# A two-layer trunk with top-2-of-8 experts on one core: the eight ranked experts run in the order of 64, 96, 64, 96, 64, 128, 96 and 32 slots instead of 128 first, the ring of weight buffers is cut down only around the 128, and the router drops twenty unread products

## The chip, the core and the metric

The kernel runs on one core of a Trainium2 chip. TensorE (PE) multiplies, VectorE (DVE) and ScalarE (ACT) do the element-wise work, GpSimd (POOL) a few small things, and SyncE (SP) issues every transfer from HBM. The metric is the time of one execution in microseconds of the device, as a median over runs. All times below are microseconds (us) from the start of the profiled span.

## The reference, cut to what matters

Layer 0 is an mLSTM and differential-attention mixer with a dense SwiGLU, layer 1 a convolution module and then a mixture of experts. The change touches the last part alone, over 256 tokens of width 1024:

```python
logits = (tokens @ router_w).astype(F32)
top_vals, top_idx = lax.top_k(logits, TOP_K)        # 2 of 8 experts for each token
gates = jax.nn.softmax(top_vals, axis=-1)
...
y = (jax.nn.silu(xb @ w1[e]) * (xb @ w3[e])) @ w2[e]   # hidden width 2816, for each expert e
out = jnp.zeros((N, D), y.dtype).at[slot_tok].add(y * slot_g)
```

All eight experts have weights of 1024 x 2816 three times over, in float32, and all are read from HBM.

## The kernel before, in words

**Ranks and slots.** The router counts how many tokens chose each expert (`counted`) and sorts the experts by that count (`ranks`). The expert of rank r gets `SLOTS[r]` places for tokens; what does not fit goes to a rare path (`overflow`) that is not taken here. Only after the sort is it known which weights belong to which rank: `bases` holds the place of each rank's weights, SP loads it into a register (L2049), and every transfer of expert weights stands behind that load on SP's queue.

**Order.** `TURNS` gives the order in which ranks are worked off, `GROUPS` which neighbours have their tokens gathered in one go. In before the widths in order of time are 128, 96, 64, 96, 64, 96, 64, 32.

**Units.** Weights come in units of 1 MB (128 x 2048 float32). An expert has 33: its hidden width is cut into six blocks (five of 512 columns, one of 256), and the order is four units of the first two matrices ("up") for a block, then two units of the third matrix ("down") for the block before it; the last block has two and one. The down unit of the last block comes behind the first four up units of the next expert. So, counting units from 0, the last up unit of the first block of expert i (i from 0) is number 3 for i = 0 and 33 i + 2 for i of 1 and more.

**Two ways to multiply.** With 128 slots (class `Expert`) each half unit is split by ACT (L371, a copy in reduced form, `whi`) and DVE (L372, the rest, `wlo`), and PE does three products per weight tile. The unit's buffer is free as soon as it is split. With fewer (class `Tiled`) PE reads the unit itself in float32, in slices of 64 (`wide`) or 32 (`narrow`) places that stand beside each other in the array. With 96 places both are done: the wide slice unit by unit, and the narrow one for all four up units only when the fourth has come (`held`), so that these four stay in use until then. ACT's Silu marks the end of a block's up products: L1809 in the 128, L1916 in the others (`cv` for the wide slice, `cvt` for the narrow one).

**The ring.** `room` is the list of buffers that successive units take: six `raw`, one made of `gp` and `m4`, three of the tag `B8`, which makes ten. While no expert is split, the four pairs of `whi` and `wlo` are used as buffers too, and a fourth `B8`: fifteen. SP issues in the order of units and stops at the first one whose buffer is still in use.

**The router's unread products.** `warm(n)` issues n products of 512 columns on PE whose result nobody reads.

The work on PE, DVE and ACT stands in the order of the code (`in_order`). The functions that the change touches:

Of the kernel before, what the change touches and what calls it, by code (L numbers as in the profile page):

```python
# [19 lines left out]
P = 128  # L20
# [6 lines left out]
NE = 8  # L27
# [5 lines left out]
AHEAD = 4  # L33

SLOTS = (128, 96, 96, 96, 64, 64, 64, 32)
TURNS = (0, 1, 4, 2, 5, 3, 6, 7)
GROUPS = ((0,), (1, 2), (3, 4), (5, 6), (7,))
NV = 2


# [195 lines left out]
def build(ctx: ExitStack, tc: tile.TileContext, d, unit, dbg=None):  # L236
# [41 lines left out]
    V, A, G, PE = nc.vector, nc.scalar, nc.gpsimd, nc.tensor  # L278
# [7 lines left out]
    def warm(n, bank="mm"):  # L286

        p_ = pm(bank)
        for _ in range(n):
            mm(p_.rearrange("p (r c) -> p r c", r=4), identr, identr.unsqueeze(1).to_broadcast([P, 4, P]), True, True)  # L290
# [36 lines left out]
    room = []  # L327
# [446 lines left out]
    for j2 in range(2):  # L774
# [4 lines left out]
        for j in range(2):  # L779
            i = 2 * j2 + j  # L780
            src = pq[:, T * j : T * j + T]
            w = cw[:, 3 * i : 3 * i + 3]
# [83 lines left out]
    for j2 in range(2):  # L866
        W = split(("k", j2))
        for j in range(2):
            pk = pm()
            wstat(W[j], pk, 0, S)  # L870
            i = 2 * j2 + j
            w = cw[:, 12 + 3 * i : 15 + 3 * i]
# [57 lines left out]
    for j2 in range(2):  # L930
# [7 lines left out]
        for j in range(2):  # L938
            i = 2 * j2 + j
            rope(qs[:, T * j : T * j + T], dqT[:, i, :])  # L940
    for j2 in range(2):
        W = split(("dk", j2))
        for j in range(2):
            i = 2 * j2 + j
# [604 lines left out]


    NU = unit[("m1", 1, 0, 0)] - unit[("m1", 0, 0, 0)]
    while len(room) < NU + 8:
        room += ["raw"] * 6 + ["gp"] + ["B8"] * 3
    while len(room) < NU * (NE - 1) - 6:
        room += ["raw"] * 6 + ["w"] * 4 + ["gp"] + ["B8"] * 4
    while len(room) < NU * NE - 13:
        room += ["raw"] * 6 + ["w"] * 4 + ["B8"] * 3
    xT_ = tl([P, KT, T], "B8")
# [169 lines left out]
    with in_order():  # L1728
        N = Norms(ys, gp)
        N.y(0, 0)  # L1730
        N.y(1, 0)
        N.y(0, 1)
        r = rms_inv(N.sy[0])
        N.add(0, 0, r)
        N.add(0, 1, r)
        rms_part(xt[:, 0, :512], N.sx[0][:, 0:1])
        N.y(1, 1, True)
        rms_part(xt[:, 0, 512:], N.sx[0][:, 1:2])
        warm(6)
        b0 = turned(xt[:, 0])  # L1740
        ry = rms_inv(N.sy[1])
        N.w_(1, 1)
        warm(3)
        b1 = turned(N.w[1])
        r0 = rms_inv(N.sx[0])
        A.copy(xT_[:, 0:4, 0:P], b0[0])
        A.copy(xT_[:, 4:8, 0:P], b0[1])
        A.copy(xT_[:, 4:8, P:], b1[1])
        warm(3)
        logits(0)  # L1750
        N.add(1, 0, ry)
        rms_part(xt[:, 1, :512], N.sx[1][:, 0:1])
        N.add(1, 1, ry)
        rms_part(xt[:, 1, 512:], N.sx[1][:, 1:2])
        V.tensor_copy(xT_[:, 0:4, P:], b1[0])
        warm(2)
        logits(1)
        r1 = rms_inv(N.sx[1])
        top2(0, r0, None)
        warm(4)  # L1760
        p0 = slots(0)
        top2(1, r1, ry)
        warm(2)
        pc = counted()
        p1 = slots(1)
        ranks(pc)
        warm(2)
        g0 = Group(0)
        p0()
        p1()  # L1770
        by_rank(posr, pos)
        g0.onehot(0)
        parts(0, 0, r0)
        g0.onehot(1)
        parts(1, 0, r1)
        parts(0, 1, r0)
        parts(1, 1, r1)
        i = g0.gather(range(2), V.tensor_copy)
    fence = fence_after(*i)
    dbg("x2", xt)  # L1780
    acc = None
# [349 lines left out]
    def later(n, *fns):  # L2131
        for i, fn in enumerate(fns):
            due.setdefault(len(todo) + n + i, []).append(fn)
# [40 lines left out]
    for i in range(NE):  # L2174
        x = ex[i]
        if i == 0:
            later(2, *[partial(g0.gather, (k,), V.tensor_copy) for k in (2, 3)])
            later(5, g0.turn)
            later(7, gates, first, partial(by_rank, gtr, gt))
            later(10, too_many)  # L2180
            later(30, left)
        for j in range(6):
            for h in range(2 if j < 5 else 1):
                if few(i):
                    todo.append(([("m1", i, j, h), ("m3", i, j, h)], None, partial(x.up2, j, h)))
                else:
                    for n in ("m1", "m3"):
                        for q in range(2):
                            todo.append(([(n, i, j, h)], q, partial(x.up, j, h, int(n == "m3"), q)))
            wait = 2 if (i, j) == (last, 5) and not few(i) else 1 if (i, j) in ((0, 0), (last, 5)) else 2 if few(i) else 3  # L2190
            later(0, partial(x.act, j))
            later(wait, partial(x.turn, j), partial(x.turned, j))
            if (i, j) == (last, 1):
                later(2, row)
            if (i, j) == (last, 3):
                later(1, slot_gate, *[partial(acc_parts, t, c) for t in range(TT) for c in range(2)])
            g = group_of.get(i + 1)
            if g is not None and g != group_of[i]:
                if j == 2:
                    later(0, partial(new_group, g), *[lambda g=g, t=t: groups[g].onehot(t) for t in range(TT)])  # L2200
                    later(3, lambda g=g: groups[g].turn())
                if j == 3:
                    later(1, *[lambda g=g, k=k: groups[g].gather((k,)) for k in range(4)])
            if j:
                downs(i, j - 1)
            elif i:
                downs(i - 1, 5)
# [100 lines left out]
```

## Time and profile before

| what | us |
|---|---|
| median of 3 runs (1324.64 to 1328.2) | 1326.01 |
| the profiled execution, its own time | 1329.66 |
| its span, from the first instruction to the last | 1327.9 |
| first transfer of expert weights issued | 604.79 |
| last expert unit used by PE | 1309.24 |

A row of the timeline has the start, the length, the engine, the line, what is written and what is read, how many instructions were merged, and in brackets how long the engine had been idle and what ended it. A product in plain float32 appears as two records. In the windows, PEclk is the granted clock of TensorE as a share of 2.4 GHz, and GB/s what the core's DMA engines moved.

### The profile page before, as it was taken

Reading aid. Unit: us, or ns where it says so; the run is one execution under the profiler, and the core shown is the slowest. Engines: PE = TensorE matmul, PEld = TensorE weight load, DVE = VectorE, ACT = ScalarE, POOL = GpSimd, SP = SyncE. Lnnn points to the kernel's source line nnn. Section 1 sums busy time; section 2 is a strip of 40 time slices with the busy share of each in tenths; the row PEclk is TensorE's granted clock in tenths of the full one; section 3 lists DMA queues with packets and bytes.
Section 4 is the critical chain, followed back from the end, with each engine's and each line's share of the span. In section 5 each row is a group of like instructions: output and inputs, shape, how many; then the busy total and the mean of one; then the engine's idle time right before and its main releaser. Section 6 shows DMA issues by size and latency. Waiting matters only on the chain. (4 is left out here: it accounts for less than half of the span.)

```text
span 1327.9 us, 21579 instructions
## 1 busy us (share of the span) xinstructions
PE 1234.6 (93%) x8655; PEld 793.5 (60%) x8655; DVE 635.7 (48%) x1055; ACT 432.9 (33%) x786; POOL 33.1 (2%) x72
## 2 busy tenths in 40 slices
PE   6999999989999998997999999999999899998654
PEld 4878777789998987686777434343343333433222
DVE  4589758698886668666977211201112021120102
ACT  4553246564434553264875001120011110110101
POOL 2000001100000010001000000000000000000000
PEclk8999999999999998996999999999999999999977
DMA  8728720478987627207987899999999999999974
GB/s 329 285 99 302 298 112 5 158 299 356 354 326 310 254 69 211 77 1 289 420 336 286 348 376 416 415 418 418 417 416 415 417 416 416 416 418 418 417 315 192
DMA packets 71518, 406.35 MB, mean 306 GB/s; under 512 B 7922, under 2 KB 12274, under 8 KB 32628
## 3 DMA queue, kind: packets, MB, share of 16 engines
q1 hardware_dynamic: 71412, 404.91, 77.1%
q8 instruction: 70, 1.15, 0.3%
q14 instruction: 36, 0.29, 0.1%
HBM read 402.94 MB, written 1.93 MB: 305 GB/s over the span
## 5 line engine op out<-in xcount | busy, mean ns | idle before, releaser
L372 DVE TENSOR_TENSOR wlo<-raw,whi 128x1024 fp32r<-128x1024 f32 x154 | 185.6, 1222 | 51.7 <-ACT whi L371 51.0
L281 PE MATMUL mm<-raw,gL 128*32 128x256 f32 (+3 forms) x1200 | 185.8, 461 | 13.6 <-DMA raw<-w 11.4
L371 ACT CAST whi<-raw 128x1024 fp32r<-128x1024 f32 x154 | 159.3, 1049 | 109.3 <-PE mm L281 64.6
L281 PE MATMUL mm<-B,whi 128*128 128x256 f32 x960 | 174.7, 283 | 0.2 <-DVE B L631 0.2
L281 PEld LDWEIGHTS mm<-B,whi 128*128 128x128 f32 x960 | 149.3, 189 | 2.4 <-PE mm L281 0.6
L281 PE MATMUL mm<-B,wlo 128*128 128x256 f32 x480 | 135.5, 282 | 0.0
L281 PE MATMUL mm<-B,gL 128*32 128x256 f32 (+3 forms) x760 | 125.4, 463 | 10.8 <-DMA B<-w 10.7
L281 PEld LDWEIGHTS mm<-raw,gL 128*32 128x32 f32 (+1 forms) x1200 | 69.5, 125 | 89.7 <-issue 56.7
L1916 ACT ACTIVATE cv<-mm 64x512 f32<-64x512 f32 (+1 forms) x36 | 19.9, 554 | 311.7 <-PE mm L281 311.6
L1917 DVE TENSOR_TENSOR cv<-cv,mm 64x512 f32<-64x512 f32 (+1 forms) x36 | 23.3, 647 | 194.4 <-ACT cv L1916 194.2
L281 PE MATMUL aux<-whi,pT 128*128 128x512 f32 (+2 forms) x360 | 100.9, 445 | 0.0
L281 PEld LDWEIGHTS mm<-B,wlo 128*128 128x128 f32 x480 | 91.0, 190 | 0.0
L281 PEld LDWEIGHTS mm<-B,gL 128*32 128x32 f32 (+1 forms) x760 | 45.8, 125 | 69.6 <-issue 42.6
L281 PE MATMUL aux<-raw,pT 128*32 128x256 f32 (+1 forms) x584 | 73.0, 463 | 5.9 <-DMA raw<-w 3.7
L281 PE MATMUL aux<-wlo,pT 128*128 128x512 f32 (+2 forms) x244 | 68.2, 456 | 1.4 <-DVE wlo L372 1.1
L1933 DVE COPY pT<-aux 128x384 f32<-128x384 f32 (+4 forms) x42 | 18.3, 436 | 99.4 <-PE aux L1926 99.3
L281 PE MATMUL mm<-U,whi 128*128 128x256 f32 (+1 forms) x240 | 64.9, 332 | 0.0
L281 PEld LDWEIGHTS aux<-whi,pT 128*128 128x128 f32 (+2 forms) x360 | 49.0, 166 | 22.9 <-issue 12.6
L281 PE MATMUL mm<-whi,B 128*128 128x512 f32 (+1 forms) x192 | 59.7, 389 | 1.2 <-DVE B L1630 1.2
L281 PE MATMUL mm<-whi,gL 128*32 128x256 f32 (+3 forms) x316 | 53.8, 453 | 5.3 <-DMA whi<-w 5.3
L281 PE MATMUL mm<-wlo,gL 128*32 128x256 f32 (+3 forms) x316 | 54.2, 465 | 0.5 <-DMA wlo<-w 0.4
L281 PEld LDWEIGHTS aux<-raw,pT 128*32 128x32 f32 (+1 forms) x584 | 25.2, 119 | 47.7 <-issue 37.7
(456 smaller groups left out, 1863.0 us busy)
## 6 DMA issues: line engine op xcount, KB each, us to landing
raw<-w SPq DMA_DIRECT2D x234, 1024.0 KB, 7.7
B<-w SPq DMA_DIRECT2D x69, 1024.0 KB, 13.7
whi<-w SPq DMA_DIRECT2D x56, 512.0 KB, 14.0
wlo<-w SPq DMA_DIRECT2D x56, 512.0 KB, 12.8
gp<-w SPq DMA_DIRECT2D x17, 512.0 KB, 10.2
m<-w SPq DMA_DIRECT2D x17, 512.0 KB, 10.1
B<-hd SPq DMA_DIRECT2D x24, 142.0 KB, 4.6
raw<-w SPq DMA_DIRECT2D x4, 512.0 KB, 6.6
```

What stands on the lines that cost most here:

```text
L281: PE.matmul(out, lhsT, rhs, start=start, stop=stop)
L371: A.copy(hi, rq)
L372: V.tensor_tensor(lo, rq, f(hi), ALU.subtract)
L1916: A.activation(s, p_[:64, :w], AF.Silu)
L1917: V.tensor_tensor(s, s, p_[64:, :w], ALU.mult)
L1933: V.tensor_copy(h[:, :o], pt[:, :o])
```

## The change

```diff
 SLOTS = (128, 96, 96, 96, 64, 64, 64, 32)
-TURNS = (0, 1, 4, 2, 5, 3, 6, 7)
-GROUPS = ((0,), (1, 2), (3, 4), (5, 6), (7,))
+TURNS = (4, 1, 5, 2, 6, 0, 3, 7)
+GROUPS = ((0,), (1, 2), (3, 4), (5,), (6, 7))
...
-    while len(room) < NU + 8:
+    whole = NU * TURNS.index(SLOTS.index(P))
+    while len(room) < whole - 30:
+        room += ["raw"] * 6 + ["w"] * 4 + ["gp"] + ["B8"] * 4
+    while len(room) < whole + NU + 8:
         room += ["raw"] * 6 + ["gp"] + ["B8"] * 3
-    while len(room) < NU * (NE - 1) - 6:
-        room += ["raw"] * 6 + ["w"] * 4 + ["gp"] + ["B8"] * 4
     while len(room) < NU * NE - 13:
         room += ["raw"] * 6 + ["w"] * 4 + ["B8"] * 3
...
-        warm(6)
         b0 = turned(xt[:, 0])
         ry = rms_inv(N.sy[1])
         N.w_(1, 1)
-        warm(3)
         b1 = turned(N.w[1])
...
-        i = g0.gather(range(2), V.tensor_copy)
+        i = g0.gather(range(2))
...
         if i == 0:
-            later(2, *[partial(g0.gather, (k,), V.tensor_copy) for k in (2, 3)])
-            later(5, g0.turn)
-            later(7, gates, first, partial(by_rank, gtr, gt))
-            later(10, too_many)
-            later(30, left)
+            later(0, partial(g0.gather, (2, 3)))
+            later(2, g0.turn)
+            later(5, gates, first, partial(by_rank, gtr, gt), too_many)
+            later(15, left)
```

Six of the seven calls of `warm` between the last layer's end and the counts go, with 6, 3, 3, 2, 4 and 2 products; the one of two products behind `ranks` stays. The code of `counted` itself is the same in both. NU is 33, so `whole` is 165, the first unit of the 128 but for the order of one: the ring has fifteen buffers up to unit 140, ten from there to unit 220, then thirteen. Before, it had ten up to unit 55, then fifteen, and thirteen from unit 240.

On SP's queue, at the first expert. Names are the buffer (`raw`, `gp` and `m4`, `B8`, `whi` and `wlo`), `w` the weights in HBM; the rows named ISA prepare an address. Before, the 128 and its ring of ten:

```order
L346 DMA raw2_1117_6040<-w 128x2048
L339 ISA
L339 DMA gp_1127_6076<-w 128x1024
L339 ISA
L339 DMA m4_1128_6077<-w 128x1024
L346 ISA
L346 DMA B8_1134_6125<-w 128x2048
```

In the change, the 64 and its ring of fifteen:

```order
L344 DMA raw2_1085_5929<-w 128x1024
L339 ISA
L339 DMA whi_1086_5932<-w 128x1024
L339 ISA
L339 DMA wlo_1087_5933<-w 128x1024
L339 ISA
L339 DMA whi_1090_5950<-w 128x1024
```

Behind the six `raw` units there now stand four units in `whi` and `wlo` before `gp` and `m4` come; before, these were where the split halves went.

On SP's queue, at the last `B8` units of the last expert, with the semaphores that each load waits for. DMAHW0 to DMAHW7 are those of the transfers, which take them in turn, PE_49 is that of TensorE's products; `blocks` belongs to the rare path. Before:

```order
L346 DMA B8_1863_10279<-w 128x2048 [waits DMAHW2_49]
L346 ISA
L346 DMA B8_1865_10294<-w 128x2048 [waits DMAHW3_49,PE_49]
L2078 TENSOR_LOAD blocks_1076_5881 [waits DVE_49]
L2078 ISA x2
L346 ISA
L346 DMA B8_1869_10311<-w 128x2048 [waits DMAHW4_49,DMAHW2_49,PE_49]
L346 ISA
L346 DMA raw_1872_10334<-w 128x2048 [waits DMAHW5_49]
```

In the change:

```order
L346 DMA B8_1846_10218<-w 128x2048 [waits DMAHW4_49]
L346 ISA
L346 DMA B8_1848_10239<-w 128x2048 [waits DMAHW5_49,PE_49]
L346 ISA
L346 DMA B8_1849_10241<-w 128x2048 [waits DMAHW6_49,PE_49]
L346 ISA
L346 DMA raw_1851_10256<-w 128x2048 [waits DMAHW7_49,PE_49]
```

Before, the third of these units (number 255) waits for the transfer of the first (number 253, on DMAHW2) and for PE: it is put into the same buffer, two units later. In the change no unit there waits for a transfer other than the eighth before it; the three (251 to 253) reuse buffers of 24 and 14 units earlier.

On PE, in the router. `identr` marks the unread products, `cst` and `x` or `xn` the transposes of the tokens, `rwg` the products with the router's weights, `sel` the counts. Before:

```order
L281 MATMUL mm_1037_5715<-identr_119_522 128x512 x6
L574 MATMUL aux_1038_5722<-cst_3_66,x_1_64 128x128 x4
L281 MATMUL mm_1044_5737<-identr_119_522 128x512 x3
L574 MATMUL aux_1045_5741<-cst_3_66,xn_1018_5689 128x128 x4
L281 MATMUL mm_1051_5758<-identr_119_522 128x512 x3
L281 MATMUL mm_1006_5674<-rwg_953_5372,B8_994_5662 128x8 x8
L281 MATMUL mm_1054_5777<-identr_119_522 128x512 x2
L281 MATMUL mm_1007_5675<-rwg_953_5372,B8_994_5662 128x8 x8
L281 MATMUL mm_1059_5798<-identr_119_522 128x512 x4
L281 MATMUL mm_1060_5803<-sel_999_5667,cst_3_66 128x8
L281 MATMUL mm_1061_5812<-identr_119_522 128x512 x2
L281 MATMUL mm_1062_5815<-sel_999_5667,one_7_74 128x8 x2
```

In the change:

```order
L574 MATMUL aux_1037_5715<-cst_3_66,x_1_64 128x128 x4
L574 MATMUL aux_1043_5730<-cst_3_66,xn_1018_5689 128x128 x4
L281 MATMUL mm_1006_5674<-rwg_953_5372,B8_994_5662 128x8 x8
L281 MATMUL mm_1007_5675<-rwg_953_5372,B8_994_5662 128x8 x8
L281 MATMUL mm_1055_5780<-sel_999_5667,cst_3_66 128x8
L281 MATMUL mm_1056_5789<-sel_999_5667,one_7_74 128x8 x2
L281 MATMUL mm_1057_5792<-sel_999_5667,cst_3_66 128x8
```

The counts (`one`) now stand directly behind the last `sel` product, and nothing stands between the two products with the router's weights.

## Rows read from the trace of the kernel before

**Rows 1.** Windows of the experts' stretch; engines' busy time, PEclk, DMA share, GB/s.

```profile
606.00:680.00 74.00, 63.40 (x275) 50.93 (x276) 59.76 (x87) 51.06 (x61) 4.04 (x11) 0.89 1.01 407
680.00:780.00 100.00, 99.97 (x686) 59.03 (x688) 44.13 (x48) 38.09 (x57) 0.00 (x0) 1.00 0.80 311
780.00:1266.00 486.00, 464.70 (x3531) 187.41 (x3531) 78.73 (x149) 53.85 (x122) 0.00 (x0) 0.99 1.02 417
1266.00:1309.00 43.00, 25.42 (x281) 11.10 (x273) 4.76 (x11) 3.44 (x8) 0.00 (x0) 0.76 0.79 324
```

**Rows 2.** Timeline of SP's queue; the time at which transfers were issued.

```profile
604.79 2.02 SPq L344 DMA_DIRECT2D raw<-w  x4
...
747.50 19.15 SPq L346 DMA_DIRECT2D raw<-w  x6
...
860.71 9.13 SPq L346 DMA_DIRECT2D raw<-w  x6
...
1203.51 9.37 SPq L346 DMA_DIRECT2D raw<-w  x6
...
1266.32 17.13 SPq L346 DMA_DIRECT2D B<-w  x3
```

**Rows 3.** Waits of SP's queue, 680 to 720: total, times, longest.

```profile
SPq L346 <- DVE wlo L372: 31.4, 10, 5.2
```

**Rows 4.** The same, 720 to 760.

```profile
SPq L346 <- PE mm L281: 21.5, 4, 11.8
```

**Rows 5.** Timeline of ACT: first split, then Silus at the ends of blocks.

```profile
608.77 1.04 ACT L371 CAST whi<-raw 128x1024 fp32r<-128x1024 f32 x1 [10.24 <-DMA raw<-w]
...
634.29 0.60 ACT L1809 ACTIVATE cv<-mm 128x512 f32<-128x512 f32 x1
...
645.75 0.59 ACT L1809 ACTIVATE cv<-mm 128x512 f32<-128x512 f32 x1
...
729.78 0.59 ACT L1916 ACTIVATE cv<-mm 64x512 f32<-64x512 f32 x1 [6.17 <-PE mm L281]
...
762.75 0.59 ACT L1916 ACTIVATE cv<-mm 64x512 f32<-64x512 f32 x1 [14.87 <-PE mm L281]
766.39 0.38 ACT L1916 ACTIVATE cvt<-mm 64x256 f32<-64x256 f32 x1 [3.05 <-PE mm L281]
...
824.43 0.59 ACT L1916 ACTIVATE cv<-mm 64x512 f32<-64x512 f32 x1 [12.50 <-PE mm L281]
...
894.28 0.59 ACT L1916 ACTIVATE cv<-mm 64x512 f32<-64x512 f32 x1 [10.41 <-PE mm L281]
```

**Rows 6.** Timeline of PE in the last expert and at its end.

```profile
1227.41 1.92 PE L281 MATMUL mm<-raw,gL 128*32 128x256 f32 x28 [1.39 <-DMA raw<-w]
1229.97 1.94 PE L281 MATMUL aux<-raw,pT 128*64 128x512 f32 x8 [0.64 <-DMA raw<-w]
...
1287.98 1.07 PE L281 MATMUL mm<-B,gL 128*32 128x256 f32 x4 [4.10 <-DMA B<-w]
...
1309.24 1.07 PE L281 MATMUL aux<-raw,pT 128*32 128x256 f32 x16 [1.53 <-SPq L2079]
```

**Rows 7.** Waits of PE, 600 to 640.

```profile
PE aux L1817 <- DVE cv L1810: 2.1, 1, 2.1
```

**Rows 8.** Timeline of PE in the router.

```profile
594.37 1.85 PE L281 MATMUL mm<-rwg,B 128*128 128x8 f32 x16
...
596.62 2.24 PE L281 MATMUL mm<-rwg,B 128*128 128x8 f32 x16
...
600.85 1.20 PE L281 MATMUL mm<-identr 128*128 128x512 f32 x2
601.85 0.85 PE L281 MATMUL mm<-sel,one 128*128 128x8 f32 x4
```

**Rows 9.** Windows of two us around the router; columns as in rows 1.

```profile
596.00:598.00 2.00, 2.00 (x17) 1.91 (x17) 1.26 (x7) 1.70 (x4) 0.55 (x1) 0.98 0.00 0
598.00:600.00 2.00, 2.00 (x8) 1.81 (x8) 0.90 (x6) 0.53 (x1) 0.00 (x0) 0.50 0.00 0
...
618.00:620.00 2.00, 2.00 (x6) 1.61 (x5) 1.93 (x2) 0.84 (x1) 0.00 (x0) 0.50 1.02 430
...
622.00:624.00 2.00, 2.00 (x14) 1.73 (x13) 0.17 (x1) 1.01 (x3) 0.00 (x0) 1.00 0.97 391
```

More of the change, by code (lines that the diff above doesn't have):

```diff
@@ L1748, in build @@
         A.copy(xT_[:, 4:8, P:], b1[1])
-        warm(3)
         logits(0)
@@ L1755, in build @@
         V.tensor_copy(xT_[:, 0:4, P:], b1[0])
-        warm(2)
         logits(1)
@@ L1759, in build @@
         top2(0, r0, None)
-        warm(4)
         p0 = slots(0)
         top2(1, r1, ry)
-        warm(2)
         pc = counted()
```

## The prediction

> **What bounds the kernel now.** I read the windows of the experts' stretch first, then SP's queue, its waits, and last the marks that ACT leaves at the ends of blocks. The windows [rows 1] show a stretch bound by transfers: from 780 to 1266 the core moves 417 GB/s without a break. It has two holes. From 680 to 780 it moves 311 GB/s, which is (417 - 311) / 417 x 100 = 25.4 us of lost transfer time, with PE busy throughout; from 1266 to 1309 it moves 324 GB/s with PE busy 25 of 43 us, so there neither is full. What is lost in a hole is never won back, because all later units queue behind it.
>
> The pace comes from SP's queue [rows 2]: from 860.71 to 1203.51 it goes nine times round the ring of fifteen, so a unit takes 342.80 / 135 = 2.54 us and an expert of 33 units 83.8. The first half unit, issued at 604.79, is met by ACT at 608.77 [rows 2, 5]: 4.0 us for half a unit, of which 1.27 is the data; I take 2.6 of the rest as latency. I call unit n **due** at 604.8 + 2.6 + 2.54 (n + 1), the time at which it would land if no hole opened, and **late** is what comes after that.
>
> The last up unit of the last expert's first block (unit 233, due 1201.8) arrives at 1227.4 [rows 6]: 25.6 late, the first hole to a few tenths. Unit 255 arrives at 1288.0 [rows 6] where 1257.6 + 25.6 = 1283.2 was to be had, and the last one, 263, at 1309.2 against 1278.0 + 25.6 = 1303.6. So the second hole costs 5.6, and the loss of both is 31.2.
>
> **Where the holes come from.** SP waits for DVE's splits from 680 to 720 [rows 3] and for PE from 720 to 760 [rows 4]: the ring of ten is full. The Silus [rows 5] say how late PE is. The 128's first block ends at 634.29, unit 3 being due at 617.6: 16.7 late. The next expert's first block ends at 729.78, 95.5 later, where transfers need 32 units or 81.3: now 31.0 late (unit 35 is due at 698.8). The place that binds is in this 96: its four up units stay held until the narrow slice is done, and with ten buffers units 53 to 55 need those of its third block. They were issued just behind its Silu of 766.39 [rows 5]; the six `raw` that begin at 747.50 end at 766.65 [rows 2]. Issued at 766.4 and 4.0 on the way, unit 53 lands 25.8 behind its due 744.6: this is the hole. So the loss is the lateness at the end of that first block less 31.0 - 25.6 = 5.4, as long as a 128 is followed by a 96 in a ring of ten and PE never idles there. The second hole is unit 255 in the buffer of unit 253: the three `B` take 17.1 us to issue at 1266.32 [rows 2].
>
> **The change, part by part.** *The first five experts.* The 64 takes PE 894.28 - 824.43 = 69.9 from first block to first block [rows 5], less than 83.8: hidden behind transfers. The 96 takes 824.43 - 729.78 = 94.7 [rows 5]: it falls 10.9 behind and the next 64 gives 13.9 back, which the ring of fifteen bore without a hole after 780 [rows 1]. So the five cost nothing, and PE reaches the 128 with nothing in arrears. The tighter ring from unit 141 on meets a 64 there; cost nothing, and up to 2 if it does not hold.
>
> *The 128, now sixth.* Its first block has four units of PE work at 645.75 - 634.29 = 11.5 in all [rows 5], which can begin 2.3 after the first of them lands (one half split: 1.04 on ACT [rows 5], a little more on DVE). The fourth lands 7.6 after the first, so the block ends 2.3 + 11.5 - 7.6 = 6.2 late, instead of 16.7. To the next first block it was 95.5. Now 2.1 goes, since the first transposes stand two steps later and no longer wait [rows 7]; one down unit of the 64 before it comes in, 1.9 [rows 6], and four return products, by the same row 1.94 / 8 x 4 = 1.0: 96.3. The 96 behind it thus ends its first block 6.2 + 96.3 - 83.8 = 18.7 late, and the hole is 18.7 - 5.4 = **13.3** in place of 25.6: **12.3 won**. Bounds: none of the additions and no wait, 10.4; the wait kept and 2 us of buffer trouble, 17.4.
>
> *After it.* The 96 begins 5.4 late and ends 16.3 late. In the last expert a pair of up units takes 1.92 and a little, a down unit 1.07 [rows 6], so a block is done in some 6.5 against 15.2 of transfers: the arrears are gone after two of six blocks.
>
> *The second hole.* No unit of the last expert takes a buffer two units back any more: **5.6 won**; at least 0, if another buffer binds there.
>
> *The router.* Two of the dropped products, 1.2 us, stood between the last `sel` and the counts, which began at 601.85 [rows 8], and the bases wait for the counts. I take **1.0 won**. The others stood in gaps. At best one product with the router's weights moves forward as well, by its 1.85 [rows 8], so 2.9 won; at worst the clock falls before both of these and they take twice their time, 3.9 more, so 2.9 lost. The row shows the clock at full up to 598 and at half from there, although eight of the unread products were still to come, and full again by 624 after steady work [rows 9]. The Trainium skill (TensorE: Matmul & The Clock Gate, What's actually happening) says that the low clock is the default and activity lifts it, which speaks against dropping them; by it the worst case here, 2.9 lost, would stand in place of 1.0 won, and the sum would be 3.9 more.
>
> *The rest.* The first six units come as halves, issued at 0.5 us each [rows 2] against 1.27 of data: hidden. The bookkeeping of the rare path comes sooner, on a DVE that is busy 79 of 486 us, and the 128's high halves are copied by an ACT busy 54 of 486 [rows 1]: hidden; uncovered, each would be under 2 us.
>
> **Sum.** 12.3 + 5.6 + 1.0 = 18.9 us. The span goes from 1327.9 to 1309.0. The profiled execution took 1329.7, 3.7 more than the median of 1326.0; taken off the median, 18.9 gives **1307.1**.
>
> **The rivals.** *The hole only moves.* The 128 is as late in the sixth place as in the first, because the return products and the gathering crowd DVE, which in the first place was busy 60 of 74 us [rows 1]. It would have to lose 12.3 us more in 33 units. Then only the second hole and the router are won: 1326.0 - 6.6 = 1319.4. Against it: 16.7 of the old lateness was there before the second block began, and came from the router.
>
> *Nothing is won.* As above, and the last expert also finds a buffer that holds it up, since its ring shrinks to thirteen and then to six `raw` as before: 1326.0 - 1.0 = 1325.0. For it: thirteen buffers begin already in the last 96. Against it: that expert needs PE for less than half of the time.
>
> *Slower: the first expert runs at half clock.* Without the unread products PE enters the 64 cold, and waiting for weights keeps it so. At half clock that expert takes 2 x 69.9 = 139.7 against 83.8, 55.9 late. Fifteen buffers can hide some 26 (thirteen units of 2.54, less 7 for the pair in use and the latency); the other 30 are a new hole, and 1307.1 + 30 = 1337. It decides from 26 + 18.9 = 45 of lateness on, four fifths of the expert at half clock. For it: the clock was at half from 598 to about 622. The Trainium skill's rule named above would bring it about. Against it: it rose while PE had only just become busy at half clock [rows 9], and a 64 at half clock would keep PE busy without a gap.
>
> *More is won.* The first hole closes altogether, since a 128's buffers are free once they are split: 1307.1 - 13.3 = 1293.8. Against it, the 96 behind it holds its units as before.
>
> **How the numbers follow.** The forecast has 0.68, and its own range is 1301 to 1314 (the bounds of the first hole and of the router, and 2 us for the tail behind the last unit). The hole only moves: 0.11. Nothing won: 0.09. Slower: 0.05. More won: 0.07. The range from 1299 to 1320 leaves out the last three. What a measurement of this kernel can tell from no change is about 0.3%, or 4 us: faster 0.68 + 0.11 + 0.07 = 0.86, same 0.09, slower 0.05.
>
> **What would show it.** Right: 417 GB/s from soon after the first issue to the middle of the sixth expert; one hole of about 13 us there, with SP waiting for PE in the third block of the 96; none in the last expert; first issue at about 604; PE waiting for transfers in the first expert. Wrong: holes in the first five experts (fifteen buffers too few, or the clock at half), a hole of 25 in the sixth, or a PE that does not catch up in the 32, so that the end is set by PE.

## The result, and the profile after

The changed kernel takes 1312.5 us (median of 4 runs, 1312.2 to 1313.4), the kernel before on the same chip 1327.1. The ratio is 0.9893, with a 95% interval from 0.9875 to 0.9911: 14.6 us faster, where 18.9 was forecast. The profiled execution has a span of 1311.6 against 1327.9, which is 16.3 less; that of the kernel before was 2.6 slower than its median, so a difference read from the two profiles comes out larger than that of the medians.

The windows of the experts' stretch in the changed kernel (busy time of PE, PEld, DVE, ACT, POOL; PEclk, DMA share, GB/s):

```profile
604.00:680.00 76.00, 70.17 (x304) 29.98 (x305) 10.51 (x40) 15.14 (x35) 2.08 (x9) 0.91 1.02 407
680.00:780.00 100.00, 95.64 (x806) 39.14 (x802) 14.08 (x25) 6.37 (x13) 0.00 (x0) 1.00 1.02 416
780.00:1030.00 250.00, 246.11 (x1716) 99.05 (x1715) 47.00 (x86) 35.73 (x76) 0.00 (x0) 0.99 1.02 416
1030.00:1120.00 90.00, 88.76 (x411) 69.61 (x410) 77.29 (x80) 69.04 (x87) 0.00 (x0) 1.00 1.00 406
1120.00:1180.00 60.00, 60.00 (x483) 29.44 (x483) 17.16 (x24) 10.47 (x16) 0.00 (x0) 1.00 0.77 311
1180.00:1260.00 80.00, 73.11 (x811) 32.94 (x809) 13.24 (x26) 7.92 (x17) 0.00 (x0) 0.97 1.01 413
1260.00:1295.00 35.00, 21.95 (x253) 10.55 (x249) 4.76 (x11) 3.46 (x8) 0.00 (x0) 0.74 0.87 358
```

The hole that stood at 680 to 780 [rows 1] is gone from there: the five experts ahead of the 128 run at 416 GB/s. A hole with the same 311 GB/s, but 60 long, stands at the 128's end and in the 96 behind it. The last stretch has 358, where it was 324, but its window runs on past the last transfer. The first row below is the part of it up to 1286, in the changed kernel; the second is the kernel before, in its second hole:

```profile
1260.00:1286.00 26.00, 17.28 (x184) 8.22 (x184) 4.25 (x9) 3.19 (x7) 0.00 (x0) 0.70 1.01 421
1276.00:1286.00 10.00, 4.93 (x34) 1.62 (x34) 1.49 (x3) 0.25 (x1) 0.00 (x0) 0.66 0.34 125
```

The second hole is gone. Within the first hole two stretches of 20 stand out in the changed kernel:

```profile
1120.00:1140.00 20.00, 20.00 (x155) 12.34 (x153) 9.16 (x10) 6.99 (x9) 0.00 (x0) 1.00 0.55 213
1160.00:1180.00 20.00, 20.00 (x176) 8.21 (x170) 3.86 (x7) 0.97 (x2) 0.00 (x0) 1.00 0.78 315
```

Four views give the sizes. SP's queue (start, time, line, transfers issued):

```profile
601.65 9.36 SPq L344 DMA_DIRECT2D raw<-w  x12
...
1123.39 17.80 SPq L346 DMA_DIRECT2D raw<-w  x6
...
1154.43 19.15 SPq L346 DMA_DIRECT2D raw<-w  x6
1173.79 0.33 SPq L339 DMA_DIRECT2D whi<-w  x1
```

The waits of that queue from 1120 to 1180 (total, times, longest):

```profile
SPq L346 <- PE mm L281: 33.6, 6, 11.8
SPq L346 <- DVE wlo L372: 7.2, 3, 2.7
```

ACT's marks: the first split of the 128, and Silus at the ends of first and third blocks:

```profile
1024.71 1.99 ACT L371 CAST whi<-B 128x1024 fp32r<-128x1024 f32 x2 [2.00 <-DMA B<-w]
...
1039.09 0.59 ACT L1804 ACTIVATE cv<-mm 128x512 f32<-128x512 f32 x1
...
1136.71 0.59 ACT L1911 ACTIVATE cv<-mm 64x512 f32<-64x512 f32 x1 [6.17 <-PE mm L281]
...
1173.32 0.38 ACT L1911 ACTIVATE cvt<-mm 64x256 f32<-64x256 f32 x1 [3.05 <-PE mm L281]
```

And PE where it meets units 260, 262 and 263 in the last expert (the first row is merged from several units and begins with 260):

```profile
1283.91 3.14 PE L281 MATMUL mm<-raw,gL 128*32 128x128 f32 x58 [2.13 <-DMA raw<-w]
...
1288.88 1.07 PE L281 MATMUL aux<-raw,pT 128*32 128x256 f32 x16 [0.65 <-DMA raw<-w]
1292.83 1.38 PE L281 MATMUL aux<-raw,pT 128*32 128x256 f32 x16 [2.88 <-SPq L2074]
```

The first hole opens in two steps. The queue stops inside the six `raw` of 1123.39, at the first unit that needs a buffer of the 96's own first block: it goes out at 1138.56, behind the Silu of 1136.71. It stops again inside the six of 1154.43, at the first unit (218) that needs one of the third block: it goes out at 1171.53, while the narrow slice of that block is being done.

By the rule of the prediction unit n is now due at 601.65 + 2.6 + 2.54 (n + 1). PE meets unit 260 at 1283.91 where 1267.2 was due: a first hole of **16.7**, for 25.6 before. It meets unit 262 at 1288.88 where 1272.3 was due, 16.6 late, so nothing new opens up to there. Only the last unit, 263, met at 1292.83 where 1274.8 was due, is 18.0 late: **1.3** more than unit 260, where the second hole cost 5.6 before. Why this one unit comes late is not shown. (The expectations below have 16.8 for the first hole and take the rest, 1.2, for a second hole at the last ring of six.) The first issue is 3.1 earlier than in [rows 2]. The sum is 8.9 + 5.6 - 1.3 + 3.1 = 16.3, which is the difference of the spans.

### The profile page after: what moved, and what is told of

Same layout as the page of the kernel before. It is cut to its first block, busy times and chain, and to the rows that moved or that the text cites. A ratio compares the mean times of both kernels' runs of the same rounds, so it can differ in the third digit from the quotient of the medians.

```text
span 1311.6 us, 21530 instructions
## 1 busy us (share of the span) xinstructions
PE 1232.6 (94%) x8635; PEld 792.7 (60%) x8635; DVE 633.5 (48%) x1051; ACT 434.4 (33%) x790; POOL 32.1 (2%) x72
## 5 line engine op out<-in xcount | busy, mean ns | idle before, releaser
L372 DVE TENSOR_TENSOR wlo<-raw,whi 128x1024 fp32r<-128x1024 f32 x152 | 182.8, 1222 | 52.3 <-ACT whi L371 50.3
L281 PE MATMUL mm<-raw,gL 128*32 128x256 f32 (+3 forms) x1280 | 181.4, 459 | 11.6 <-DMA raw<-w 11.5
L281 PE MATMUL mm<-B,gL 128*32 128x256 f32 (+3 forms) x648 | 109.2, 465 | 6.7 <-DMA B<-w 6.7
L281 PE MATMUL aux<-raw,pT 128*32 128x256 f32 (+1 forms) x608 | 80.5, 470 | 6.9 <-DMA raw<-w 4.0
L281 PEld LDWEIGHTS mm<-B,gL 128*32 128x32 f32 (+1 forms) x648 | 39.5, 125 | 54.8 <-issue 38.0
L1928 DVE COPY pT<-aux 128x256 f32<-128x256 f32 (+4 forms) x42 | 18.3, 436 | 94.7 <-PE aux L1921 94.5
L281 PE MATMUL aux<-B,pT 128*32 128x256 f32 (+2 forms) x368 | 59.2, 491 | 2.8 <-DVE pT L1928 1.8
L281 PEld LDWEIGHTS aux<-raw,pT 128*32 128x32 f32 (+1 forms) x608 | 28.2, 120 | 50.0 <-issue 37.6
L281 PE MATMUL mm<-U,wlo 128*128 128x256 f32 (+1 forms) x160 | 52.8, 330 | 0.0
```

Of the source, the lines that this page charges most:

```text
L281: PE.matmul(out, lhsT, rhs, start=start, stop=stop)
L372: V.tensor_tensor(lo, rq, f(hi), ALU.subtract)
L1928: V.tensor_copy(h[:, :o], pt[:, :o])
```

## The experiments

One rule divides each profile into three parts. The *start* runs to the first weight transfer and is counted from the eight products of the gain's row that PE does ahead of the router (their own place wanders from 571.6 to 578.3 over the profiles, so a span alone says little). The *loss* is the start of the last unit's products less the first issue, less 2.6 + 2.54 x 264 = 673.2. The *tail* behind is 17.8 to 19.3 everywhere. For the changed kernel: 601.65 - 576.44 = 25.2, and 1292.83 - 601.65 - 673.2 = 18.0.

| kernel | order of slots | start | loss | median us | ratio to before, 95% |
|---|---|---|---|---|---|
| before | 128, 96, 64, 96, 64, 96, 64, 32 | 29.7 | 31.3 | 1327 to 1328 | |
| after | 64, 96, 64, 96, 64, 128, 96, 32 | 25.2 | 18.0 | 1312.5 | 0.9893 [0.9875, 0.9911] |
| before_no_unread | as before | 25.2 | 29.8 | 1327.7 | 1.0003 [0.9983, 1.0023] |
| after_with_unread | as after | 27.7 | 16.1 | 1313.7 | 0.9888 [0.9861, 0.9916] |
| ring_early | as after | 25.2 | 26.5 | 1321.2 | 0.9943 [0.9922, 0.9964] |
| whole_then_32 | 64, 96, 64, 96, 64, 96, 128, 32 | 25.7 | 16.4 | 1309.1 | 0.9868 [0.9840, 0.9896] |
| ring_after_first_block | as after | 25.5 | 16.7 | 1313.5 | 0.9901 [0.9876, 0.9926] |
| before_end_ring | as before | 29.7 | 22.6 | 1321.9 | 0.9957 [0.9935, 0.9980] |
| slow_between_fast | 96, 64, 96, 64, 128, 64, 96, 32 | 25.2 | 0.8 | 1295.6 | 0.9759 [0.9734, 0.9785] |
| slow_pair_late | 64, 96, 64, 128, 64, 96, 96, 32 | 25.2 | 3.9 | 1300.6 | 0.9810 [0.9781, 0.9838] |
| ring_both_ends | as after | 25.3 | 11.8 | 1307.1 | 0.9839 [0.9820, 0.9859] |
| slow_between_fast_plain | 96, 64, 96, 64, 128, 64, 96, 32 | 25.2 | -0.8 | 1294.5 | 0.9745 [0.9722, 0.9768] |
| slow_between_fast_whole | the same | 25.2 | -0.9 | 1294.4 | 0.9754 [0.9736, 0.9771] |
| order_plain_with_unread | the same | 27.7 | -0.2 | 1296.6 | 0.9766 [0.9739, 0.9794] |

Two profiles with the same order and rings differ by 1.9 in the loss (after and after_with_unread). In before and before_end_ring, which have the same order and the same ring up to the last but one expert, the first hole is 25.6 and 22.7. So only differences above some 3 are read from a pair of profiles.

### The unread products

**before_no_unread**, the edit in the kernel before:

```diff
-        warm(6)
         b0 = turned(xt[:, 0])
...
-        warm(4)
         p0 = slots(0)
```

(six such lines in all).

> The kernel before with the six groups of unread products in the router taken out and nothing else. The first weight transfer was issued at 604.79 in the profile of before and at 601.65 in that of after, though in after the work ahead of the router ended 1.3 later. Theory (the whole of this gain comes from the unread products): first issue 3 to 4.5 earlier, both holes as before (25.6 and 5.6), and the time 3 to 4.5 lower, 1322.6 to 1324.1. Rival one (my forecast's term, only the two products between the last selection and the counts matter): 1.0 lower, 1326.1. Rival two (something else in the change made the router shorter, such as the turned-round ranking of slots): no change. The clock should stay at its full level until after both products with the router's weights, whose 32 rows should take about 3.6 in all.

Measured: no change, 1.0003. The profiled execution has the first issue 4.5 earlier behind the gain's row, and both products with the router's weights in one go at the full clock. A row of PE's timeline:

```profile
588.60 3.64 PE L281 MATMUL mm<-rwg,B 128*128 128x8 f32 x32
```

But this execution was the fastest of 12 (1320.8, the others up to 1332.1), and the mean granted clock of the 12 is 0.968 where the 21 of before have 0.972. What the router wins here is not in the time; where it goes in the usual executions is not shown.

**after_with_unread**, the same six lines put into the changed kernel.

> The changed kernel with the six groups of unread products put back: the new order and ring alone. Theory: first issue 3 to 4.5 later than 601.65, the remaining holes as in after (16.8 and 1.2), the time 1315.5 to 1317.0. Rival (the unread products cost 1.0): 1313.5. Rival two (the clock in the first expert is worth something): with the clock at full level sooner the 64's first block ends earlier, but as transfers set the pace there, nothing of it should show in the time.

Measured: 1313.7, 1.2 above after, with a first issue 2.5 later behind the gain's row and a loss that came out 1.9 smaller. Neither the 3 to 4.5 nor the 1.0 can be told by it, since loss and time wander by as much. What it does show is that the new order and ring alone, 0.9888, give the gain of the whole change, 0.9893, within the intervals.

**order_plain_with_unread**, the last of the runs, puts them into the best order found below, where no hole hides an earlier start.

> The order 96, 64, 96, 64, 128, 64, 96, 32 with the ring rules of the changed kernel and the six groups of unread products put back. So far the profiles say that with the unread products the first weight transfer is issued 27.7 to 29.7 behind the products with the gain's row (three profiles), without them 25.2 to 25.7 (nine); the times say 0 to 1 for the same edit, each known to some 2.7 only. In this order no hole of more than some 3 hides an earlier start. Theory one (what the profiles show is worth its full size): 2.5 to 4.5 above the same order without them, 1297.0 to 1299.0. Theory two (my forecast's 1.0, or nothing): 1294.5 to 1295.5.

Measured: 1296.6 against 1294.5, 2.1 more; in the profiles 27.7 against 25.2, 2.5 more, with losses 0.6 apart. The intervals of the two times overlap, so the times alone do not show a cost; the profiles do: the unread products cost **2.5** there, the lower end of the first theory, more than my 1.0. The gain's row and the router of this kernel:

```profile
578.30 1.04 PE L514 MATMUL mm<-cst,gpc 128*128 128x128 f32 x8
...
597.57 1.85 PE L281 MATMUL mm<-rwg,B 128*128 128x8 f32 x16
599.27 0.71 PE L281 MATMUL mm<-identr 128*128 128x512 f32 x2
599.82 1.84 PE L281 MATMUL mm<-rwg,B 128*128 128x8 f32 x16
```

The same two places in slow_between_fast_plain, the same order without unread products:

```profile
577.00 1.03 PE L514 MATMUL mm<-cst,gpc 128*128 128x128 f32 x8
...
594.03 3.64 PE L281 MATMUL mm<-rwg,B 128*128 128x8 f32 x32
```

The last product with the router's weights ends 599.82 + 1.84 - 578.30 = 23.4 behind the gain's row with the unread products and 594.03 + 3.64 - 577.00 = 20.7 without them, 2.7 apart. So the whole cost has arisen by then, from the groups ahead of and between these products. The clock is at its full level in both groups here, so it is the unread products themselves that stand in the way. In the profiles of before [rows 8] and before_end_ring it had fallen in the second group (2.24 and 2.22), and the start is 2.0 longer again.

### The ring of ten in the 96

**ring_early**:

```diff
-    while len(room) < whole + NU + 8:
+    while len(room) < whole + NU - 12:
```

> The changed kernel, with the ring of ten ended some twenty units earlier, so that the 96 behind the 128 has a ring of thirteen from its fourth unit on. PE has no wait in after from the 128 to the 32, so its marks should stand where they stood. Theory (ring of ten in the 96, with PE late): the third block of the 96 ended at 1173.3, the fourth at 1190.6, the fifth at 1207.1; with the new ring the units that wait for these are 221, 227 and 234, which would land 9.2, 11.2 and 9.9 behind their due time, so the hole is 11.2 instead of 16.8 and the time 5.6 lower, 1306.9. Rival (the hole belongs to PE or to the splits, and more buffers only move the waiting): 1312.5, same hole.

Measured: 1321.2, 8.7 slower than after, the loss 26.5. I had overlooked what the new ring puts first. SP's queue in this kernel:

```profile
1089.80 18.77 SPq L346 DMA_DIRECT2D raw<-w  x6
1124.42 0.33 SPq L339 DMA_DIRECT2D whi<-w  x1
...
1128.84 0.34 SPq L339 DMA_DIRECT2D whi<-w  x1
...
1130.98 0.33 SPq L339 DMA_DIRECT2D whi<-w  x1
...
1141.04 0.33 SPq L339 DMA_DIRECT2D whi<-w  x1
```

and its waits from 1100 to 1145:

```profile
SPq L339 <- DVE wlo L372: 14.3, 3, 12.5
SPq L339 <- PE aux L281: 13.3, 3, 8.0
```

Units 201 to 204 ask for buffers that still hold halves of the 128, and the queue, which issues in order, stands still until PE has read them. From 1100 to 1120 the core moves 232 GB/s and from 1120 to 1140 159, where the changed kernel has 360 and 213: that is 6.1 and 2.6 more lost, the 8.7. The run does not test the ring, so it was made again one round later.

**ring_after_first_block**, with `NU - 2` in that line.

> The changed kernel, with the ring of ten ended one round earlier, behind unit 210. The run before this one ended it behind unit 200, and there the queue of SP stopped for some 14 us at the fourth unit of the 96, whose buffer was one that the 128 still needed for its halves. Here those buffers are asked for only behind the first block of the 96, when the 128 is done with them. Theory (ring of ten in the 96, with PE late and without a wait until the 32): the marks of PE stand where they stood in after; unit 207 still lands 8 late, unit 221 then 9.2, unit 227 9.7 and unit 233, which waits for the fifth block, 12.5: a hole of 12.5 in place of 16.8, the time 4.3 lower than after. Rival (more buffers only move the waiting): hole 16 to 17, the time of after.

Measured: 1313.5, the time of after. Two windows of it:

```profile
1160.00:1180.00 20.00, 20.00 (x172) 8.08 (x166) 4.10 (x7) 0.97 (x2) 0.00 (x0) 1.00 1.01 421
...
1260.00:1295.00 35.00, 18.70 (x221) 9.32 (x221) 3.54 (x9) 1.70 (x4) 0.00 (x0) 0.71 0.75 309
```

The third block of the 96 no longer stops transfers (421 GB/s, 315 in after), but the last stretch falls from 358 to 309 (from 1260 to 1270 it is 241, where the changed kernel has 421). As every round behind moved by ten units, the last three `B` came to units 254 to 256, and the third needs the buffer of unit 254: the second hole of before was back, by my own edit. **ring_both_ends** takes it away again:

```diff
-    while len(room) < NU * NE - 13:
+    while len(room) < NU * NE - 20:
```

> The changed kernel with the ring of ten ended behind unit 210, as in the run before, and the last ring of six begun at unit 250 as well, so that no unit of the last expert takes a B two places ahead. In the run before, less was lost in the 96 (389 to 421 GB/s from 1140 on, against 315 to 404 in after), but three B fell on units 254 to 256, the last of them waited for unit 254, and the last stretch fell to 309 GB/s. Theory (the ring of ten in the 96 is worth some 4, and the three B took it back): first hole 12 to 13, 1 to 2 at the end, the time 4 lower than after, about 1308. Rival (what is won in the 96 is lost in the last expert whatever its ring, as PE comes to it as late as before): the time of after, 1312 to 1314.

Measured: 1307.1, 5.4 below after, the loss 11.8 instead of 18.0. The theory holds: the ring of ten in the 96 costs 4 to 6 of the first hole, and PE's lateness alone does not bring it back later. Most of the 11.8 that is left arises where transfers wait for the 96's first block (222 GB/s from 1120 to 1140, for 213 in after).

### The last ring

**before_end_ring**, in the kernel before:

```diff
-    while len(room) < NU * (NE - 1) - 6:
+    while len(room) < NU * (NE - 1) - 17:
```

> The kernel before with its ring of fifteen ended one round earlier and nothing else, so that its last three B stand at units 251 to 253 instead of 253 to 255 and none waits for the unit two places ahead of it. Theory: the last expert's hole shrinks from 5.6 to the 1.2 that after has left at its last ring of six, and the time is 4.4 lower than before. Rival (the last expert is held up anyway, by PE or by the ring of six): no change. The first hole stays 25 to 26 in both.

Measured: 1321.9, 5.5 below before (interval 2.7 to 8.6). The last stretch, where [rows 1] has 324:

```profile
1266.00:1300.00 34.00, 25.25 (x261) 11.87 (x261) 4.76 (x11) 3.43 (x8) 0.00 (x0) 0.65 0.92 378
```

PE where it meets unit 233, as in [rows 6]:

```profile
1224.62 1.92 PE L281 MATMUL mm<-raw,gL 128*32 128x256 f32 x28 [1.52 <-DMA raw<-w]
```

The loss fell by 8.7. Of this 2.9 are of the first hole: unit 233 was due at 604.98 + 2.6 + 594.4 = 1201.9 and is 22.7 late, where before has 25.6. The edit does not touch that part; the 128's first Silu stands 631.73 - 604.98 = 26.8 behind the first issue here, in before 29.5. The expectation that the first hole stays at 25 to 26 missed. The last unit is 22.6 late, no more than unit 233: the second hole is gone whole, and the last ring of six, which this kernel has too, costs nothing.

### What opens the first hole

**whole_then_32**:

```diff
-TURNS = (4, 1, 5, 2, 6, 0, 3, 7)
+TURNS = (4, 1, 5, 2, 6, 3, 0, 7)
```

> The changed kernel with the 128 and the last 96 exchanged: 64, 96, 64, 96, 64, 96, 128, 32; the ring of ten moves with the 128. Theory (the hole comes from the 96 behind the 128, which holds its four up units until the narrow slice is done): behind the 128 stands a 32, which holds nothing; unit 240 waits for the first block of the 32, at about 1217.5, and lands some 5 behind its due time, and the 96 in the ring of ten may cost 0 to 3. The holes together 5 to 9 instead of 18.0, the time 1300 to 1304. Rival (a 128 is late by its own work, whatever stands behind it): a hole of about 17 remains, 1312. Rival two: as the 128 stands nearer to the end, PE is still behind when the last unit lands, and the tail behind it grows; then PE and not a transfer sets the end.

Measured: 1309.1, with a loss of 16.4 where 5 to 9 was expected. My theory that the held units of the 96 *behind* the 128 make the hole is not enough. The windows of this kernel:

```profile
1030.00:1110.00 80.00, 80.00 (x714) 33.80 (x714) 14.51 (x28) 13.51 (x33) 0.00 (x0) 1.00 0.95 387
...
1130.00:1230.00 100.00, 99.40 (x548) 76.70 (x550) 84.14 (x85) 69.56 (x79) 0.00 (x0) 1.00 0.96 366
```

PE is busy without a gap through the 96 and the 128, now in this order, and transfers starve in both. The sum of the pair is the same: the 96 needs 10.9 more of PE than of transfers and the 128 some 14, and what the ring can't bear is lost, whichever of the two comes first. That is an account so far; the next runs test it.

**slow_between_fast** follows from that: every slow expert gets a 64 or the 32 behind it.

```diff
-TURNS = (4, 1, 5, 2, 6, 0, 3, 7)
-GROUPS = ((0,), (1, 2), (3, 4), (5,), (6, 7))
+TURNS = (1, 4, 2, 5, 0, 6, 3, 7)
+GROUPS = ((0,), (1,), (2, 3), (4, 5), (6, 7))
...
+    while len(room) < NU * (NE - 1) - 6:
+        room += ["raw"] * 6 + ["w"] * 4 + ["gp"] + ["B8"] * 4
-    while len(room) < NU * NE - 13:
+    while len(room) < NU * NE - 18:
```

> The changed kernel in the order 96, 64, 96, 64, 128, 64, 96, 32, with the slots gathered in groups that begin behind a 64, a ring of fifteen again behind the ring of ten, and the last ring of six a little earlier. Theory (what opens a hole is the lateness of PE that neighbours add up; a slow expert between two fast ones stays within what the ring bears): 64s give back 7.5 to 9 of what a 96 adds, so PE comes to the 128 9 to 10 late and leaves it some 24 late; unit 166 lands 4 to 6 late, and no hole opens in the last 96 with its fifteen buffers. Holes together 5 to 8 instead of 18.0; the time 10 to 13 lower than after, 1300 to 1303. Rival one (the 128 makes its hole alone, by its splits and the ring of ten): hole 16 to 17, the time of after. Rival two (a 96 cannot begin: its first block needs more of a cold PE than a 64's): a new hole in the first two experts, and the time no better than after.

Measured: 1295.6, 16.9 below after, a loss of 0.8. The theory had the direction, but its size, 5 to 8, was too large. **slow_pair_late** has the same ring rules, `TURNS = (4, 1, 5, 0, 6, 2, 3, 7)` and the groups of after but `(3, 4), (5,)` for its 128.

> The changed kernel in the order 64, 96, 64, 128, 64, 96, 96, 32, with the same rings as the order 96, 64, 96, 64, 128, 64, 96, 32. Theory (lateness adds up over neighbours): PE comes to the 128 about 8 late and leaves it 22 late, the 64 behind it holds nothing, and at most 0 to 3 are lost there; but the two 96s behind each other add up to some 30, of which a ring of fifteen bears 24 to 26 where its units are held, so a second hole of 4 to 8 opens in the second of them. Holes together 5 to 10, the time 8 to 13 lower than after. Rival (the hole is the 128's own): 16 to 17 are lost at the 128, and the time is that of after or higher.

Measured: 1300.6, a loss of 3.9. Its windows put it where the theory wants it:

```profile
870.00:965.00 95.00, 94.86 (x442) 72.31 (x441) 79.66 (x76) 67.09 (x73) 0.00 (x0) 1.00 1.00 412
...
1150.00:1278.00 128.00, 116.18 (x1270) 52.78 (x1258) 22.80 (x44) 12.71 (x28) 0.00 (x0) 0.95 0.99 400
```

At the 128 (417 - 412) / 417 x 95 = 1.1 is lost, in the stretch of the second 96 and the 32 (417 - 400) / 417 x 128 = 5.2. The two are more than the loss of 3.9, so the windows say where it is lost and not how much. A 128 between two 64s makes no hole by itself, and two 96s do.

**slow_between_fast_plain** leaves the ring rules of the changed kernel as they are, only `TURNS` and `GROUPS` differ.

> The order 96, 64, 96, 64, 128, 64, 96, 32 and its groups alone, with the ring rules of the changed kernel as they are: a ring of thirteen behind the ring of ten up to unit 258. Theory (the order does it, the ring of fifteen behind the 128 does not): 1295 to 1298, with 415 GB/s and more in every stretch but the one behind the 128. Rival (the last 96 needs the fifteen buffers): a hole of 4 to 8 in the last 96, 1300 to 1304.

Measured: 1294.5. The order alone does it. Its windows and its last unit:

```profile
604.00:680.00 76.00, 75.85 (x618) 34.75 (x620) 12.48 (x40) 11.89 (x25) 3.04 (x10) 0.93 1.02 408
680.00:930.00 250.00, 250.00 (x1824) 101.55 (x1822) 42.93 (x83) 34.41 (x81) 0.00 (x0) 1.00 1.02 417
930.00:1050.00 120.00, 117.59 (x552) 85.37 (x549) 92.06 (x90) 77.00 (x86) 0.00 (x0) 1.00 1.01 414
1050.00:1240.00 190.00, 182.42 (x1510) 75.01 (x1508) 33.08 (x63) 21.87 (x50) 0.00 (x0) 0.99 1.02 415
1240.00:1272.00 32.00, 21.32 (x245) 10.74 (x245) 4.76 (x11) 3.45 (x8) 0.00 (x0) 0.73 1.00 414
```

```profile
1274.57 1.07 PE L281 MATMUL aux<-raw,pT 128*32 128x256 f32 x16 [1.47 <-SPq L2074]
```

From the first issue to the last unit transfers now run at their pace throughout, so the order has nothing more to give. **slow_between_fast_whole** tries the start of that stretch. It is slow_between_fast, with its rings, and one edit more:

```diff
-                        r = raw(None, unit_of(key[1], key[0], *key[2:]), two=n < 4)
+                        r = raw(None, unit_of(key[1], key[0], *key[2:]), two=n < 1)
```

> The order 96, 64, 96, 64, 128, 64, 96, 32 with the ring of fifteen, and of its first six units only the first two as halves (the changed kernel issues six units as twelve halves, in 9.36 where twelve at 0.5 would take 6, and moves 344 GB/s in the first 20 from the first issue). Theory (each transfer waits for the one eight before it, so twelve halves keep less in flight than whole units): the first unit behind the six is issued 1 to 1.5 sooner after the first issue, the time 1 to 1.5 lower, about 1294.3. Rival (the first units wait for buffers that the router frees, or for the data anyway): no change, 1295.6.

Measured: 1294.4, 1.2 below slow_between_fast, as the theory has it, but 0.9754 and 0.9759 have intervals that overlap almost whole. The first unit behind the six is issued 29.8 behind the gain's row instead of 35.6, and the last one is met 672.3 behind the first issue instead of 674.0; slow_between_fast_plain, which issues twelve halves, has 672.4. So the earlier issue brings at most 1 to 2, and theory and rival can't be told apart.

## Why the prediction came out as it did

The direction, the mechanism and the place of the holes were right, and 1312.5 lies in both ranges, 1.5 inside the upper end of the forecast's own. The gain was 14.6 instead of 18.9. In the profiles the first hole gave 3.4 less than forecast, the router 2.1 more and the last unit cost 1.3; that two of the errors partly cancel is luck.

*The first five experts cost nothing*: right. 416 GB/s from 680 to 1030; the tighter ring cost nothing there.

*The 128, now sixth: a hole of 13.3*: the mechanism was right, the size was not; it measured 16.7, so 8.9 was won, not 12.3. It lies inside the bounds that the prediction gave, 10.4 to 17.4, near the upper one. Two terms were too small, both by 1 to 2.
- "The block ends 6.2 late" measured 1039.1 - 1031.0 = 8.1 (its last up unit is 167). Of the 1.9 between, 1.4 is that unit 164, the first of the block, lands at 1024.7 and not at its due 1023.3; over five profiles of this order the 128's first Silu stands 436.0 to 437.5 behind the first issue, so this comes and goes.
- "95.5 to the next first block", from which I made 96.3, measured 1136.7 - 1039.1 = 97.6. The 95.5 were counted between two Silus [rows 5], and the first of them came late. ACT's timeline of the kernel before, ahead of that Silu:

```profile
630.49 1.28 ACT L1992 ACT_TABLE_LOAD   x1
631.84 0.20 ACT L1992 ACTIVATE gg<-gg 128x2 f32<-128x2 f32 x1
631.95 1.03 ACT L371 CAST whi<-raw 128x1024 fp32r<-128x1024 f32 x1
633.00 1.28 ACT L1809 ACT_TABLE_LOAD   x1
```

PE had done 54 products by 633.6, where the wait of [rows 7] begins; 48 are the block and six products, 1.4, are already of the next one, so the block ended at 632.2 and its Silu stood 2.1 behind it, with two table loads ahead of it. A cycle measured from a late mark comes out short by as much.

Both terms add up: 8.1 + 97.6 - 83.8 = 21.9 late instead of 18.7, and less the 5.2 that the ring bears (5.4 in the prediction) this is the 16.7.

The start of the sum was uncertain too. The prediction's 25.6, and the 16.7 by which it found the 128's first block late, come from one profile. before_end_ring has 22.7 for the same hole, and its 128's first Silu, like that of before_no_unread (623.25 - 596.79 = 26.5), stands some 3 earlier behind the first issue than in before. So 8.9 is won between the two profiles, and 6 against the other. And the prediction read the issue of unit 53 from the end of a merged row, 766.4; the row of that one transfer has 764.60. That its landing came out at the 25.6 of the hole was partly luck. What the prediction also left out is that transfers wait for the 96's first block as well; the third only comes last.

*What opens the hole*: the prediction puts the place that binds in the 96 behind the 128, and it named the condition, "as long as a 128 is followed by a 96 in a ring of ten". ring_both_ends shows the ring's part, and slow_between_fast and slow_pair_late that the hole goes away with a 64 on either side of the 128. But it saw one pair only: whole_then_32 loses nearly as much, 16.4, with the 96 ahead of the 128. The lateness of neighbours adds up, and the held units are only the place where it comes out.

*The second hole: 5.6 won*: right. The unit two places ahead was the cause, as before_end_ring and, against my will, ring_after_first_block show, and nothing is left of the hole up to unit 262. The 1.3 that the last unit then comes late is no part of it, as before_end_ring ends with the same ring of six and does not have it.

*The router: 1.0 won*: too small. In the profile the first issue came 3.1 earlier, and 4.5 counted from the gain's row; where it can be read best the unread products cost 2.5 in the profile (order_plain_with_unread), and about 2 more in an execution whose clock falls in the second group. The step that failed is "the others stood in gaps". They filled the gaps and more: with them PE is busy for all 14 us from 590 to 604 in the profile of before, and the first product with the router's weights begins 594.37 - 575.11 = 19.3 behind the gain's row, where the changed kernel has 593.47 - 576.44 = 17.0. Of the two products that the 1.0 was for, no effect can be seen. My lower bound supposed that without them the clock falls ahead of the router's products. It did not, as the row of the changed kernel shows:

```profile
593.47 3.64 PE L281 MATMUL mm<-rwg,B 128*128 128x8 f32 x32
```

All ten profiles without the unread products have these 32 at 3.64 to 4.13, and of the four with them two have a slow second group. In the changed kernel the granted clock is 1.00 up to 596, 0.79 from 596 to 598 and 0.50 behind that, so it falls behind these products and not ahead of them. The Trainium skill (TensorE: Matmul & The Clock Gate, What's actually happening) has the low clock as the default that activity lifts. This trace does not contradict that, but the 2.9 lost that the prediction drew from it did not come: the clock was at its full level at the router's products without the unread ones.

*The rivals*: that the hole only moves, or that nothing is won, is refuted by the first hole of 16.7 and by units 260 and 262, which show no second one. The first expert at half clock did not come: the granted clock is 0.93 from 612 to 640 and 0.98 from 640 to 680, and PE waits for transfers there (5.7 in all from 640 to 700). More is won: not here, but slow_between_fast reaches a loss of nothing by another order.

What stays open: why the kernel before gains nothing in time without its unread products, though its profile does; why the last unit of the changed kernel lands late; and what the moved bookkeeping of the rare path and the copies by ACT are worth, which no run changes alone.

## What to carry to other kernels

Where each stage has its own balance of transfers and compute, write down for each what compute needs over what transfers take, and order the stages so that no two slow ones stand together: the ring has to bear the sum of a run of neighbours, not the worst stage. An edit of a ring moves every later unit to another buffer, so look at the end of the program and at buffers lent to other work, too. Count a cycle from the engine that does the work, not from a mark on another engine that may come late, and split a span into start, loss and tail before two executions are compared.

## What the runs showed of the hardware that was not expected

- The part of the program that no edit here touches ends, by the gain's row, at 571.6 to 578.3 after the start of the span in fourteen profiles: 6.7, more than most of the effects looked for.
- With the same instructions ahead of it, the second group of router products took 2.24 and 2.22 in two profiles (before, before_end_ring) and 1.84 in two others (after_with_unread, order_plain_with_unread): the granted clock fell at about 598 in the first two, in after_with_unread only at about 605.
- Six units issued as eight transfers instead of twelve let the next transfer start 5.8 earlier behind the gain's row (slow_between_fast_whole and slow_between_fast), and the last unit was met only 1.7 earlier behind the first issue.
- With the same code ahead of it, the first hole of the old order was 25.6 in one profile and 22.7 in another (before, before_end_ring).
